# A two-layer decoder trunk on one core: the first stage's normalised input made by ScalarE, two weight pieces shifted, six more filling products

## The chip, the cores and the metric

The kernel runs on one core of one Trainium2 chip. The metric is device time in microseconds (us) of one execution, lower is better. An execution's time is the span from the first to the last instruction and a little around it: the profiled execution took 977.15 us, of which the span is 975.3 us.

## The reference

One sequence of 256 tokens, width 1024, goes through two layers. Each layer is a half-step gated feed-forward network (FFN), an attention and a second half-step FFN. Before each of them the residual is normalised and modulated with numbers made from a conditioning vector c. The part that the change touches is the very first of these:

```python
def rms_norm(x, g):
    xf = x.astype(jnp.float32)
    y = xf * lax.rsqrt(jnp.mean(xf * xf, axis=-1, keepdims=True) + EPS)
    return (y * g.astype(jnp.float32)).astype(x.dtype)

def modulate(h, shift, scale):
    return h * (1 + scale[:, None, :]) + shift[:, None, :]

def swiglu(h, w_in, w_out):
    g, u = jnp.split(h @ w_in, 2, axis=-1)
    return (jax.nn.silu(g) * u) @ w_out

c_act = jax.nn.silu(c)
mod = c_act @ ada_w[layer] + ada_b[layer]
sh1, sc1, g1, sh2, sc2, g2, sh3, sc3, g3 = jnp.split(mod, N_MOD, axis=-1)
h = modulate(rms_norm(x, norm_g[layer, 0]), sh1, sc1)
x = x + 0.5 * g1[:, None, :] * swiglu(h, ffn_w_in[layer, 0], ffn_w_out[layer, 0])
```

All weights are float32 in HBM, some 260 MB with the matrices that make `mod`.

## The kernel before, in words

**Split products.** Every large product is made of three matmuls (`mm3`, line 410). A float32 number is written as a high part rounded to TensorE's format (fp32r) plus a low part, the remainder rounded. The three are high weight times high input, low weight times high input, high weight times low input; low times low is dropped. The names are `wh`, `wl` for a weight piece and `HH`, `HL` for the normalised input. Each of the three has 128 weight columns as its stationary operand and 256 tokens as the moving one.

**The stream of weight pieces.** All weight matrices form one list of pieces of 128 x 1024 numbers (or less), loaded in order by SP's queue into six buffers `raw` (`w_dma`, line 287). ScalarE (ACT) rounds a piece to `wh` (`cp_part`, line 298, six buffers); VectorE (DVE) subtracts, `wl = raw - wh` (`sub_part`, line 310, five buffers); TensorE (PE) uses them up. A piece is 24 matmuls. A `raw` buffer is free, and its next transfer issued, when its `wl` has been made. A dictionary `shift` (line 268) starts a few pieces, the first ones of a stage, 16 numbers (64 bytes) further on in their buffer.

**The modulation numbers.** The rows of the matrices that give `mod` come in units of 1 MB, `ada`, into three buffers. `ada_block` (line 196) handles half a unit, 128 outputs: one DVE instruction multiplies it by `cact` and sums (with a second one, DVE_READ_ACCUMULATOR, that reads the sum out). For a scale the block then makes `A = (1 + scale) * g`, the norm's weight times the modulation. In the first stage this is done for each column at once, by a DVE instruction on 128 x 1 numbers. After the second half of a unit SP is asked for the next one.

**The first stage.** The first FFN starts before anything is known: x, c and the weights are still arriving. So its first 16 column blocks (`win0`, K0 = 4 groups of gate and up) go over all 8 chunks of the contraction, `for k in range(NC)` in `ffn` (line 576), with all 8 PSUM banks as accumulators, `pf0` to `pf7`. A turn k has 48 matmuls and needs two weight pieces, 2k and 2k+1, one `ada` unit (scale and shift of chunk k) and the chunk's input. `make_h` (line 467) makes that: DVE writes `ht = x * A * r`, where r is the reciprocal root mean square; ACT writes `HH = ht + shift`, rounded; DVE writes `HL = (ht + shift) - HH`. The first piece's `cp_part` stands ahead of the loop (line 929).

**After the loop.** ACT loads the table for Silu, rounds two further pieces, and then reads the accumulators: `sg = silu(pf0)` on ACT, then `hf = sg * pf1` on DVE (`evac`, line 562), and so on for four pairs. The next group's accumulators `pg4` and `pu4` lie in the banks of `pf0` and `pf1` (one pool of four banks, tag `mm`), so they can't be written before `sg` and `hf` have read these.

**The order.** Each engine runs its instructions in the order of the program. In the first stage that order is the order of the code. After it a planner decides (class `InOrder`, line 54, and `bg`, line 378): a rough clock for each engine, with costs per instruction, places the rounding, subtracting and `ada_block` work between the others. A change in the first stage thus changes the planner's clocks and, a little, what it places where later on. PE's order is written out by hand and has no such freedom.

**Filling products.** `warm(n)` (line 896) issues n products of a constant tile with itself on PE, which nothing reads, while PE would wait; six of them stand just ahead of the first stage.

Of the kernel before, what the change touches and what calls it, by code (L numbers as in the profile page):

```python
# [10 lines left out]
F32 = mybir.dt.float32  # L11
F32R = mybir.dt.float32r
BF16 = mybir.dt.bfloat16
AF = mybir.ActivationFunctionType
# [89 lines left out]
def trunk(ctx, tc, a, out):  # L104
# [91 lines left out]
    def ada_block():  # L196

        u, i = divmod(ada_done[0], 2)
        if u >= len(ada_list):
            return  # L200
        ada_done[0] += 1
        t = ada_tiles[u]
        m, j = ada_list[u][i]
        if m not in mods:
            mods[m] = [mod_col(), None]
        mt = mods[m][0]
        col = V_ADAB + 2 * u + i
        dve.tensor_tensor_reduce(
            t[:, i], t[:, i], cact, 1.0, vecs[:, col:col + 1], ALU.mult, ALU.add,
            accum_out=mt[:, j:j + 1])  # L210
        kind = m[1] % 3 if m[0] != "kv" else m[1]
        if kind != 0 and m[1] != 5:
            if mods[m][1] is None:
                mods[m][1] = mod_col()
            mx = mods[m][1]
            js = (j, j + 1) if m == (0, 1) else ((j - 3, j + 1) if j % 4 == 3 else None)
            if js is not None:
                js = slice(*js)
                if kind == 1:
                    gc = V_KVN if m[0] == "kv" else V_NORM + (m[0] * 3 + m[1] // 3) * NC  # L220
                    dve.scalar_tensor_tensor(
                        mx[:, js], mt[:, js], 1.0, vecs[:, gc + js.start:gc + js.stop],
                        op0=ALU.add, op1=ALU.mult)
                else:
                    dve.tensor_scalar_mul(mx[:, js], mt[:, js], 0.5)
        if i == 1:
            ada_dma()
# [45 lines left out]
        shift[first] = 16  # L273
    first = next(p for p, v in enumerate(pieces) if v[0].tensor is a["wlast"].tensor)
    shift.update({p: 32 if p > first else 16 for p in range(first, len(pieces))})
    gated = [None]
    raws, his, los = [], [], []
    taken = [0]
# [19 lines left out]
    def cp_part():  # L298

        u = len(his)  # L300
        n = pieces[u][2]
        act.t = max(act.t, used[u - NHI] if u >= NHI else 0.0)
        raw = raws[u]
        if u >= len(pieces) - 6:
            gated[0](raw[:, :n])
        wh = wp.tile([P, WB], F32R, tag="wh", name="wh")[:, shift.get(u, 0):]
        act.plainly(lambda: act.copy(wh[:, :n], raw[:, :n]))
        his.append(wh)
# [158 lines left out]
    def make_h(k, r, m):  # L467

        A, sh = mods[m[0]][1], mods[m[1]][0]
        t = kp.tile([P, S], F32, tag="ht", name=f"ht{k}")  # L470
        dve.scalar_tensor_tensor(t, x[k], A[:, k:k + 1], r, op0=ALU.mult, op1=ALU.mult)
        hh, hl = hn[k]
        act.activation(hh, t, AF.Identity, bias=sh[:, k:k + 1])
        return lambda: dve.scalar_tensor_tensor(hl, t, sh[:, k:k + 1], hh.bitcast(F32),
                                                op0=ALU.add, op1=ALU.subtract)

    class MakeH:


# [68 lines left out]
    def ffn(l, i, kind, m, nxt, at=2):  # L548
# [24 lines left out]
        if (l, i) == (0, 0):  # L573
            banks = ([mmbank(f"pf{b}") for b in range(4)] + [sbank(f"pf{b}") for b in range(4, 6)]
                     + [abank("pf6"), bbank("pf7")])
            for k in range(NC):
                if k:
                    ada_block()
                    cp_part()
                    ada_block()  # L580
                f = make_h(k, kind, m)
                sub_part()
                cp_part()
                f()
                sub_part()
                blk = take("win0")
                for b in range(4 * K0):
                    mm3(banks[b // 2][:, (b % 2) * 256:(b % 2) * 256 + 256], blk(b * P), hn[k],
                        k == 0 and b % 2 == 0, k == NC - 1)
            table(AF.Silu)  # L590
            cp_part()
            sub_part()
            cp_part()
            sub_part()
            mode[0] = "run"
            for j in range(K0):
                if j < 2:
                    evac(banks[2 * j], banks[2 * j + 1])
                    if j == 0:
                        flush()  # L600
                        flush()
                else:
                    later(2 * j - 2, lambda j=j: evac(banks[2 * j], banks[2 * j + 1]))
            j0 = K0
        elif kind == "late":
            banks = [mmbank("lg0"), mmbank("lg1"), sbank("lu0"), sbank("lu1")]
            r = None
            for kh in range(2):
                blk = take("win")
                for kk in range(4):  # L610
                    k = kh * 4 + kk
                    for b in range(4):
                        mm3(banks[b][:, :SX], blk(kk * 512 + b * P), hx[k], k == 0, k == NC - 1)
                    if k == 2:
                        r = rstd_of(AF.Silu)
                        mh = MakeH(r, m)
                    elif 2 < k < 7:
                        if k == 6:
                            cp_part()
                        mh.go(2 if k < 6 else 1)  # L620
            sub_part()
            mh.go(2)
            mode[0] = "run"
            sg = kp.tile([P, 512], F32, tag="w512a", name="sg")
            hf = kp.tile([P, 512], F32, tag="w512b", name="hf")
            cols = []

            def late_block(b):
                if b == 0:
                    cols.append(late_cols(banks))  # L630
                c = cols[0]
                t = kp.tile([P, S], F32, tag="sq", name=f"lt{b}")
                dve.tensor_tensor(t, banks[b][:, :S], r, op=ALU.mult)
                cs = slice((b % 2) * S, (b % 2) * S + S)
                if b < 2:
                    act.activation(sg[:, cs], t, AF.Silu, bias=c[:, b:b + 1])
                else:
                    dve.scalar_tensor_tensor(hf[:, cs], t, c[:, b:b + 1], sg[:, cs],
                                             op0=ALU.add, op1=ALU.mult)
                if b == 3:  # L640
                    hid_out(hf)
            for b in range(4):
                later(2 + b, lambda b=b: late_block(b))
            j0 = 1
# [251 lines left out]
    def warm(n):  # L896

        pw = bbank("warm")
        for _ in range(n):
            mm(pw[:, :P], ones, ones, start=True, stop=True)  # L900
# [24 lines left out]
    ada_block()  # L925
    ada_block()
    rstd = rstd_of(None, [sq4[i][:, h * S:(h + 1) * S] for i in (0, 2) for h in range(2)])
    warm(6)
    cp_part()


# [572 lines left out]
```

## Time and profile before

| | |
|---|---|
| median of 3 runs | 973.57 us |
| the runs | 970.95, 977.09, 973.57 us |
| profiled execution | 977.15 us |
| its span | 975.3 us |
| granted TensorE clock | 0.998 (1.00 in every stretch from 10 us on) |
| busy: PE / DVE / ACT / POOL | 99% / 84% / 57% / 7% |
| 128 x 256 matmuls of fp32r, mean | 277 to 278 ns each, about 113 to 118 ns from start to start |
| first stage (turns 0 to 7) on PE | 13.8 to 60.5 us |

How to read it: matmuls are pipelined, so a row's duration (0.28 us) is longer than the distance to the next row's start, and it is the distance that counts. The same is true on DVE and ACT, by some hundredths of a microsecond: what an instruction costs in a full queue is the distance to the next start. The page's share of 99% for PE therefore doesn't say that PE is at its peak, only that something is nearly always in it.

### The profile page before, as it was taken

How to read it: one execution, taken by the hardware profiler on the slowest of the kernel's cores; microseconds unless marked ns; L12 is line 12 of the kernel's file. 1: busy time of each engine (PE TensorE's matmuls, PEld its weight loads, DVE VectorE, ACT ScalarE, POOL GpSimd, SP SyncE). 2: the span in 40 equal slices, each digit the busy share in tenths (PEclk: the TensorE clock that was granted, in tenths of full speed). 3: DMA queues.
4: the chain of work that ended last, by engine and by line, in shares of the span. 5: the costliest groups of instructions: out<-in, count | busy, mean ns of one | idle time of the engine just before them, and what ended most of it. 6: DMA issues, size and time to landing. Idle time of an engine off the chain costs nothing.

```text
span 975.3 us, 20416 instructions
## 1 busy us (share of the span) xinstructions
PE 964.5 (99%) x8076; PEld 937.8 (96%) x8076; DVE 822.0 (84%) x1372; ACT 551.3 (57%) x894; POOL 67.5 (7%) x110
## 2 busy tenths in 40 slices
PE   8999999999999999999999999999999999999997
PEld 6999999998999999999998999999998899999997
DVE  7989979989999998878889989888988799555575
ACT  5465545666787644445567554545567776555432
POOL 0000100000112000000000000000034013300000
PEclk9999999999999999999999999999999999999999
DMA  9988999968767699878959799988996337977651
GB/s 361 414 352 279 332 361 341 356 224 277 288 212 252 201 379 373 289 257 301 318 186 376 272 353 336 365 295 307 331 297 195 105 117 214 279 155 270 185 152 44
DMA packets 69473, 268.22 MB, mean 275 GB/s; under 512 B 9417, under 2 KB 10225, under 8 KB 59266
## 3 DMA queue, kind: packets, MB, share of 16 engines
q1 hardware_dynamic: 66016, 259.69, 76.3%
q0 software_dynamic: 3072, 6.92, 2.4%
q8 instruction: 63, 1.03, 0.4%
q10 hardware_dynamic: 290, 0.32, 0.1%
q14 instruction: 32, 0.26, 0.1%
HBM read 264.75 MB, written 2.66 MB: 274 GB/s over the span
## 4 chain that ended last, share of the span: by engine, by line
PE 96%; DVE 2%; ACT 1%; DMA 1%; issue 0%; POOL 0%; SPq 0%; DVEq 0%; ACTq 0%
PE po L99 25%; PE pg L99 21%; PE pu L99 21%; PE pf L99 5%; PE pv L99 5%; PE lp L99 4%; PE pqk L99 3%; PE pw L99 3%; PE lq L99 1%; PE lu L99 1%; PE lg L99 1%; PE pk L99 1%; DVE ada L99 1%; PE wb L99 1%; DMA ada<-in_ada 1%; PE sb L99 1%
## 5 line engine op out<-in xcount | busy, mean ns | idle before, releaser
L99 ACT CAST wh<-raw 128x1024 fp32r<-128x1024 f32 (+1 forms) x360 | 346.8, 973 | 213.7 <-PE pu L99 84.8
L99 DVE TENSOR_TENSOR wl<-raw,wh 128x1024 fp32r<-128x1024 f32 (+1 forms) x360 | 399.7, 1128 | 75.6 <-ACT sg L99 20.7
L99 DVE CUSTOM_DVE_ANT_0 ada<-ada,cact,vecs 128x1024 f32<-128x1024 f32 x160 | 203.5, 1279 | 0.3 <-DMA ada<-in_ada 0.3
L99 PE MATMUL pg<-HH,wl 128*128 128x256 f32 x608 | 168.8, 278 | 0.0
L99 PE MATMUL pg<-HH,wh 128*128 128x256 f32 x608 | 168.7, 278 | 0.0
L99 PE MATMUL pu<-HH,wh 128*128 128x256 f32 x608 | 168.6, 277 | 0.0
L99 PE MATMUL pu<-HL,wh 128*128 128x256 f32 x608 | 168.6, 277 | 0.0
L99 PE MATMUL pg<-HL,wh 128*128 128x256 f32 x608 | 168.6, 277 | 0.0
L99 PE MATMUL pu<-HH,wl 128*128 128x256 f32 x608 | 168.6, 277 | 0.0
L99 PE MATMUL po<-hidh,wh 128*128 128x256 f32 x528 | 146.6, 278 | 0.0
L99 PE MATMUL po<-hidh,wl 128*128 128x256 f32 x528 | 146.6, 278 | 0.0
L99 PE MATMUL po<-hidl,wh 128*128 128x256 f32 x528 | 146.6, 278 | 0.0
L99 PEld LDWEIGHTS pg<-HH,wl 128*128 128x128 f32 x608 | 114.7, 189 | 0.1
L99 PEld LDWEIGHTS pg<-HH,wh 128*128 128x128 f32 x608 | 114.2, 188 | 0.7 <-issue 0.6
L99 PEld LDWEIGHTS pu<-HH,wl 128*128 128x128 f32 x608 | 114.7, 189 | 0.0
L99 PEld LDWEIGHTS pu<-HL,wh 128*128 128x128 f32 x608 | 114.1, 188 | 0.0
L99 PEld LDWEIGHTS pg<-HL,wh 128*128 128x128 f32 x608 | 114.1, 188 | 0.0
L99 PEld LDWEIGHTS pu<-HH,wh 128*128 128x128 f32 x608 | 114.1, 188 | 0.0
L99 PEld LDWEIGHTS po<-hidh,wl 128*128 128x128 f32 x528 | 99.9, 189 | 0.0
L99 PEld LDWEIGHTS po<-hidh,wh 128*128 128x128 f32 x528 | 99.1, 188 | 0.0
L99 PEld LDWEIGHTS po<-hidl,wh 128*128 128x128 f32 x528 | 99.1, 188 | 0.0
L99 ACT CAST hidh<-hf 128x512 fp32r<-128x512 f32 x44 | 27.3, 621 | 41.2 <-DVE hf L99 41.0
(224 smaller groups left out, 1849.1 us busy)
## 6 DMA issues: line engine op xcount, KB each, us to landing
raw<-in_win SPq DMA_DIRECT2D x176, 512.0 KB, 6.9
ada<-in_ada SPq DMA_DIRECT2D x79, 1024.0 KB, 7.2
raw<-in_wout SPq DMA_DIRECT2D x48, 384.0 KB, 5.6
raw<-in_wout SPq DMA_DIRECT2D x48, 320.0 KB, 5.8
raw<-in_wqk SPq DMA_DIRECT2D x16, 512.0 KB, 5.4
raw<-in_wo SPq DMA_DIRECT2D x16, 512.0 KB, 5.1
raw<-in_wlast SPq DMA_DIRECT2D x16, 512.0 KB, 4.4
raw<-in_wv SPq DMA_DIRECT2D x8, 512.0 KB, 7.3
```

The source lines that it names most:

```text
L99: return self.tc.keep_in_program_order(f(*args, **kw))
```

## The change

Four edits, all in the first stage or ahead of it.

1. `ada_block`: for the first norm of layer 0, `A` is made by ACT (`Identity` of `mt * g + g`) and no longer by DVE.
2. `make_h_first` takes the place of `make_h` in the loop over k. ACT makes h twice: `HH`, rounded, as before, and `h` in float32. DVE then only subtracts, `HL = h - HH`, from two tiles.
3. For k = 0 one more `cp_part` stands ahead of `make_h_first`; every later rounding in the loop is thereby one piece further on than before.
4. `shift` also holds pieces 4 and 10, the first pieces of turns 2 and 5; and `warm(6)` becomes `warm(12)`.

```diff
@@ ada_block
                 if kind == 1:
                     gc = V_KVN if m[0] == "kv" else V_NORM + (m[0] * 3 + m[1] // 3) * NC
+                    g = vecs[:, gc + js.start:gc + js.stop]
+                    if m == (0, 1):
+                        act.activation(mx[:, js], mt[:, js], AF.Identity, bias=g, scale=g)
+                        return
                     dve.scalar_tensor_tensor(
-                        mx[:, js], mt[:, js], 1.0, vecs[:, gc + js.start:gc + js.stop],
-                        op0=ALU.add, op1=ALU.mult)
+                        mx[:, js], mt[:, js], 1.0, g, op0=ALU.add, op1=ALU.mult)
@@ shift
     shift.update({p: 32 if p > first else 16 for p in range(first, len(pieces))})
+    shift.update({2 * k: 16 for k in (2, 5)})
@@ beside make_h
+    def make_h_first(k, r, m):
+
+        A, sh = mods[m[0]][1], mods[m[1]][0]
+        t = kp.tile([P, S], F32, tag="ht", name=f"ht{k}")
+        dve.scalar_tensor_tensor(t, x[k], A[:, k:k + 1], r, op0=ALU.mult, op1=ALU.mult)
+        hh, hl = hn[k]
+        act.activation(hh, t, AF.Identity, bias=sh[:, k:k + 1])
+        h = kp.tile([P, S], F32, tag="sq", name=f"h{k}")
+        act.activation(h, t, AF.Identity, bias=sh[:, k:k + 1])
+        return lambda: dve.tensor_tensor(hl, h, hh.bitcast(F32), op=ALU.subtract)
@@ ffn, the first stage's loop
                     ada_block()
                     cp_part()
                     ada_block()
-                f = make_h(k, kind, m)
+                if k == 0:
+                    cp_part()
+                f = make_h_first(k, kind, m)
                 sub_part()
                 cp_part()
                 f()
@@ ahead of the first stage
-    warm(6)
+    warm(12)
```

The order that comes out of it is shown at two places. The first is DVE in the first turn and the start of the second; `ht`, `HL` and `wl` are as above, `ISA ada` is the product and sum of half a unit, `ISA modall` reads it out, and `SCALAR_TENSOR_TENSOR modall` is `A`. Before:

```order
L99 SCALAR_TENSOR_TENSOR ht0_171<-x_78,modall_91,r0_148 128x256
L99 TENSOR_TENSOR wl_174<-raw_97,wh_161 128x1024
L99 SCALAR_TENSOR_TENSOR HL_93<-ht0_171,modall_91,HH_92 128x256
L99 TENSOR_TENSOR wl_181<-raw_99,wh_178 128x1024
L99 ISA ada_101,modall_91<-ada_101,cact_89,vecs_76 128x1024
L99 ISA modall_91 128x1
L99 SCALAR_TENSOR_TENSOR modall_91<-modall_91,vecs_76 128x1
L99 ISA ada_101,modall_91<-ada_101,cact_89,vecs_76 128x1024
L99 ISA modall_91 128x1
```

And the same place in the change:

```order
L99 SCALAR_TENSOR_TENSOR ht0_179<-x_78,modall_91,r0_148 128x256
L99 TENSOR_TENSOR wl_184<-raw_97,wh_167 128x1024
L99 TENSOR_TENSOR HL_93<-h0_182,HH_92 128x256
L99 TENSOR_TENSOR wl_191<-raw_99,wh_177 128x1024
L99 ISA ada_101,modall_91<-ada_101,cact_89,vecs_76 128x1024
L99 ISA modall_91 128x1
L99 ISA ada_101,modall_91<-ada_101,cact_89,vecs_76 128x1024
L99 ISA modall_91 128x1
```

`A` has left DVE, and `HL` reads `h0`, which ACT has to make first. Every turn is changed in this way.

The second place is ACT at the end of the first stage, from the last turn's `HH` to the first read of an accumulator. `CAST` is `cp_part`, and the `raw` that it reads tells the piece. Before, piece 15 is `raw_459`, piece 16 `raw_521`, piece 17 `raw_528`, piece 18 `raw_590`:

```order
L99 ACTIVATE HH_92<-ht7_654,modall_91 128x256
L99 CAST wh_661<-raw_459 128x1024
L99 ACT_TABLE_LOAD
L99 CAST wh_717<-raw_521 128x1024
L99 CAST wh_723<-raw_528 128x1024
L99 ACTIVATE sg_729<-pf0_163 128x512
L99 CAST wh_735<-raw_590 128x1024
```

In the change piece 15 is `raw_477`, piece 16 `raw_541`, piece 17 `raw_548`, piece 18 `raw_612`:

```order
L99 CAST wh_671<-raw_477 128x1024
L99 ACTIVATE HH_92<-ht7_676,modall_91 128x256
L99 ACTIVATE h7_679<-ht7_676,modall_91 128x256
L99 CAST wh_685<-raw_541 128x1024
L99 ACT_TABLE_LOAD
L99 CAST wh_741<-raw_548 128x1024
L99 CAST wh_747<-raw_612 128x1024
L99 ACTIVATE sg_753<-pf0_169 128x512
```

The casts of pieces 15 to 17 each stand one place earlier, and the cast of piece 18 now stands ahead of `sg` on the first accumulator instead of behind it. The third place is DVE right after that, from the last `HL` of the first stage. In the change:

```order
L99 TENSOR_TENSOR HL_93<-h7_679,HH_92 128x256
L99 TENSOR_TENSOR wl_688<-raw_477,wh_671 128x1024
L99 TENSOR_TENSOR wl_743<-raw_541,wh_685 128x1024
L99 TENSOR_TENSOR wl_749<-raw_548,wh_741 128x1024
L99 TENSOR_TENSOR wl_756<-raw_612,wh_747 128x1024
L99 TENSOR_TENSOR hf_755<-sg_753,pf1_170 128x512
L99 ISA ada_532,modall_91<-ada_532,cact_89,vecs_76 128x1024
```

Before, the fourth `wl` (of piece 18) stood behind `hf`, and the first `ada` block of the next stage some fifteen rows later. PE's order is the same but for the six filling products. From here to the end DVE and SP have the same work in a slightly other order, with a few `ada` blocks placed earlier or later.

## The prediction

> **What bounds the kernel now.** I read the page's totals first, then the chain of waits, then the timeline of the first stage engine by engine, and last a table by stretches. The profiled execution took 977.15 us: a span of 975.3 us and 1.85 us around it.
>
> ```profile
> span 975.3 us, 20416 instructions
> PE 964.5 (99%) x8076; PEld 937.8 (96%) x8076; DVE 822.0 (84%) x1372; ACT 551.3 (57%) x894; POOL 67.5 (7%) x110
> ```
>
> PE sets the time nearly everywhere. Something changed in the first stage counts only if it lets PE reach the next stage earlier. The chain in order of time (start, length, engine, matmuls) shows the turns as PE has them, each counted from its third product:
>
> ```profile
> 14.79 5.73 PE pf L99 x48
> ...
> 54.99 5.69 PE pf L99 x46
> ```
>
> From 14.79 to 54.99 are seven turns of 5.74 us. Is that PE's own pace? The third product of the last turn on PE, and a whole turn on DVE (start, length, engine, operation; the distance to the next start is the cost):
>
> ```profile
> 54.99 0.39 PE L99 MATMUL pf<-HL,wh 128*128 128x256 f32 x1
> ```
> ```profile
> 49.18 1.23 DVE L99 TENSOR_TENSOR wl<-raw,wh 128x1024 fp32r<-128x1024 f32 x1
> 50.32 1.28 DVE L99 CUSTOM_DVE_ANT_0 ada<-ada,cact,vecs 128x1024 f32<-128x1024 f32 x1
> ...
> 51.64 0.16 DVE L99 SCALAR_TENSOR_TENSOR modall<-modall,vecs 128x1 f32<-128x1 f32 x1
> 51.72 1.28 DVE L99 CUSTOM_DVE_ANT_0 ada<-ada,cact,vecs 128x1024 f32<-128x1024 f32 x1
> ...
> 52.92 0.48 DVE L99 SCALAR_TENSOR_TENSOR ht<-x,modall,r 128x256 f32<-128x256 f32 x1
> 53.32 1.22 DVE L99 TENSOR_TENSOR wl<-raw,wh 128x1024 fp32r<-128x1024 f32 x1
> 54.46 0.48 DVE L99 SCALAR_TENSOR_TENSOR HL<-ht,modall,HH 128x256 fp32r<-128x256 f32 x1
> 54.93 1.23 DVE L99 TENSOR_TENSOR wl<-raw,wh 128x1024 fp32r<-128x1024 f32 x1
> ```
>
> No: PE's third product waits until `HL`, started at 54.46, is written, and DVE goes from `wl` at 49.18 to `wl` at 54.93, 5.75 us, without a gap. DVE bounds the first stage, by 0.3 us a turn over PE at 113 ns a product (48 x 0.1132 = 5.43 us). The stretches (length, PE busy and products, PEld, DVE, ACT, POOL, clock, DMA share, GB/s) show two more things:
>
> ```profile
> 50.00:60.00 10.00, 9.99 (x86) 9.79 (x86) 8.83 (x13) 6.27 (x8) 0.00 (x0) 1.00 1.02 414
> 60.52:63.37 2.85, 2.85 (x27) 2.85 (x26) 2.85 (x4) 2.57 (x5) 0.00 (x0) 1.00 1.03 411
> 64.00:106.00 42.00, 42.00 (x373) 42.00 (x373) 37.05 (x49) 24.09 (x29) 0.00 (x0) 1.00 0.80 271
> 110.00:196.00 86.00, 86.00 (x761) 86.00 (x760) 74.89 (x112) 44.48 (x63) 4.19 (x8) 1.00 0.96 353
> 318.00:326.00 8.00, 8.00 (x73) 8.00 (x72) 7.13 (x14) 5.07 (x12) 0.00 (x0) 1.00 0.39 131
> 330.00:500.00 170.00, 170.00 (x1443) 169.95 (x1442) 146.12 (x206) 87.39 (x113) 1.63 (x3) 1.00 0.89 312
> 545.00:715.00 170.00, 170.00 (x1502) 170.00 (x1501) 153.45 (x215) 85.76 (x108) 0.00 (x0) 1.00 0.91 327
> ```
>
> First, the DMA engines are full during the first stage. Second, PE has two paces for the same kind of matmul at a full clock and without a gap: 170/1502 = 113.2 ns, and 170/1443 = 117.8 ns through the second FFN. At 318 that FFN is still fast (8.00 us for some 71 products, two of the 73 being left over from ahead of the window); it changes at a wait:
>
> ```profile
> 326.03 0.28 PE L99 MATMUL pg<-HH,wh 128*128 128x256 f32 x1
> 326.19 0.39 PE L99 MATMUL pg<-HH,wl 128*128 128x256 f32 x1
> ```
>
> The slow pace costs 174 x (1 - 113.2/117.8) = 6.8 us from there to 500 alone. The three runs lie 6.1 us apart, about one such stretch, and the profiled run is at the slow end, 3.6 us above the median. So I make the sum against 977.15 and carry only the difference to the median.
>
> **The change part by part.** *DVE's turn.* `A` goes, and with it the distance from the first `ada` block to the second falls from 51.72 - 50.32 = 1.40 to what a block costs that is followed by something else, 52.92 - 51.72 = 1.20. `HL` becomes a subtraction of two tiles, for which the residual sums are the nearest row:
>
> ```profile
> 171.85 0.42 DVE L99 TENSOR_TENSOR acc<-acc,sq 128x256 f32<-128x256 f32 x1
> 172.19 0.82 DVE L99 TENSOR_TENSOR wl<-raw,wh 128x640 fp32r<-128x640 f32 x1
> ```
>
> That is 0.34 against 54.93 - 54.46 = 0.47 now. The turn is then wl 1.14, two blocks 2.40, `ht` 0.40, `wl` 1.14, `HL` 0.34, 5.42 us, where it was 5.75. PE's own 5.43 takes over: 0.31 a turn less, 2.1 us over seven.
>
> *ACT's turn.* It gains `h`, 128 x 256, bounded by `HH`'s row below (0.41 to the next start, 0.51 in all), and `A`, 128 x 1, for which the nearest row is 0.21:
>
> ```profile
> 324.40 0.21 ACT L99 COPY lcol<-lg 128x1 f32<-128x1 f32 x2
> ```
>
> With two casts of 1.04 that is 3.2 of 5.43 us. `h` is done 0.51 + 0.41 + 0.51 = 1.43 us after `ht` starts, and DVE turns to `HL` 0.40 + 1.14 = 1.54 after it: it fits by 0.1. Because the cast of the next piece stood between `HH` and DVE's second `wl`, moving the casts one place ahead also frees that step.
>
> *The start.* The extra cast stands ahead of the first `HH`:
>
> ```profile
> 11.05 1.04 ACT L99 CAST wh<-raw 128x1024 fp32r<-128x1024 f32 x1 [0.18 <-DMA raw<-in_win]
> 13.25 0.51 ACT L99 ACTIVATE HH<-ht,modall 128x256 fp32r<-128x256 f32 x1 [1.15 <-DVE ht L99]
> ```
> ```profile
> L99 SPq DMA_DIRECT2D raw<-in_win x2: 499/546/592, 2.9 to 3.6; - x2
> DMA to landing us min/median/max: 8.1/8.4/8.7
> ```
>
> Piece 1 was issued at 3.6 and landed 8.7 later, at 12.3; its cast ends at 13.3. `A` off DVE brings `ht` 0.2 forward, so `HH` could have run at 13.05 and now runs at 13.3: level with before. With `h` done 0.92 after that, at 14.2, `HL` can start where it did (14.79 less the last turn's 54.99 - 54.46, 14.26), and is 0.13 shorter; but I count half of that, since ACT is now just in time. Start: -0.07 us, bounds -0.2 and +0.3.
>
> *Filling products.* Twelve of them are 24 rows of 0.112, 2.7 us from 10.19, done at 12.9, ahead of the first `HH` (13.25), for which PE has to wait anyway:
>
> ```profile
> 10.19 1.50 PE L99 MATMUL warm<-ones 128*128 128x128 f32 x12
> ```
>
> The clock was 1.00 across the gap before, so I price them at nothing.
>
> *The shifted pieces.* The stretch at 60.52 is a shifted piece: 24 products in 2.85 us, 119 ns. Turns 2 and 5 get one such piece each. Against the fast pace that costs 24 x 5.6 ns = 0.13 us a turn; where the turn would have been slow, 48 x 4.6 ns = 0.22 can come back if the other piece turns fast. Between -0.2 and +0.13 a turn; I take +0.13, since with the slow wait gone I expect fast turns. The Trainium skill ("TensorE: Matmul & The Clock Gate", Part 2, step 1) says that PE has two independent read ports, so that loading weights doesn't slow the matmul that streams; by that an address could matter to neither, and this term would be 0. The two paces in the rows, at one form, speak against it.
>
> *What is late next.* With PE through its last turn at 14.72 + 7 x 5.43 + 0.26 + 46 x 0.1132 = 58.2 instead of 60.5, 2.3 us earlier, the next group's `pg4` and `pu4` need the banks of `pf0` and `pf1`. Before, `sg` and `hf` had read these in time:
>
> ```profile
> 53.44 0.51 ACT L99 ACTIVATE HH<-ht,modall 128x256 fp32r<-128x256 f32 x1 [3.34 <-DVE ht L99]
> 53.85 1.04 ACT L99 CAST wh<-raw 128x1024 fp32r<-128x1024 f32 x1
> 54.91 1.28 ACT L99 ACT_TABLE_LOAD   x1
> 56.20 2.00 ACT L99 CAST wh<-raw 128x1024 fp32r<-128x1024 f32 x2
> 58.11 0.59 ACT L99 ACTIVATE sg<-pf 128x512 f32<-128x512 f32 x1
> ```
> ```profile
> 59.56 0.68 DVE L99 TENSOR_TENSOR hf<-sg,pf 128x512 f32<-128x512 f32 x1
> ```
> ```profile
> 60.52 0.28 PE L99 MATMUL pg<-HH,wh 128*128 128x256 f32 x1
> ...
> 61.23 0.28 PE L99 MATMUL pu<-HH,wh 128*128 128x256 f32 x1
> ```
>
> In the change the cast of piece 18 stands ahead of `sg`. Piece 18 is the transfer issued at 48.83:
>
> ```profile
> L99 SPq DMA_DIRECT2D raw<-in_win x1: 327/327/327, 48.8 to 48.8; - x1
> DMA to landing us min/median/max: 8.9/8.9/8.9
> ```
>
> It landed at 57.7. In the change it is issued some 2 us earlier, but the engines ahead of it are full (share 1.02, 414 GB/s), and the same bytes stand ahead of it, so I expect it at 57.7 again. Then: cast until 58.75, `sg` 58.7 to 59.3, and `pg4` waits about 1.0 us. DVE's order has `wl` of piece 18 ahead of `hf` too: `wl` from 58.8, `hf` 59.95 to 60.63, and `pu4` starts at 60.65 instead of 61.23. Behind the waiting cast on ACT stand `sg` and all later casts; PE is the one who waits. Of 2.3 us, 0.6 stays.
>
> *After that* PE runs product to product (170.00 busy of 170.00), with `wl` made five pieces ahead, so 0.6 us is carried to the end; the few `ada` blocks placed elsewhere lie on a DVE busy 146 of 170. Sum: 977.15 - 0.6 = 976.6 for an execution like the profiled one, 973.57 - 0.6 = 973.0 for the median.
>
> **The rivals.** *Piece 18 is not late.* If it lands by 56, the whole 2.3 us stays: 971.3. For it: it is issued 2 us earlier. Against: the full engines. The Trainium skill ("DMA: Bandwidth & Descriptors", Where 436 GB/s comes from) has a ceiling of 435 GB/s; at that rate the bytes between 11.0 and 57.7 would be there at 55.4, an estimate, and this rival would hold. The rows have 414.
>
> *The slow stretch doesn't come.* The wait at 326 is of 0.2 us, and the order around it hardly changes, but whether the pace changes there is not in the order. Without it: 976.6 - 6.8 = 969.8. For it: the fastest run before, 970.95, can hardly have had one.
>
> *Slower: the new wait leaves PE at the slow pace.* `pg4`'s wait of 1 us is of the kind after which the pace changed at 326, and here everything from 64 to 196, at the fast pace now (42/373, 86/761), hangs on it: 128 x (117.8/113.2 - 1) = 5.2 us, median 973.0 + 5.2 = 978.2. It decides from 0.6/0.0046 = 130 products on, a tenth of the stretch. Against it: the piece at 60.52 is a shifted one and came out at the fast pace.
>
> *No change in time:* `h` late or the casts starved, DVE's turn not shorter: 973.6.
>
> **How the numbers follow.** Forecast 0.45 (973.0; its own range 970 to 977, the spread of the runs), piece 18 in time 0.15 (971.3), no slow stretch 0.15 (969.8), slow after the new wait 0.2 (978.2), no change 0.05 (973.6). The range 968.5 to 978.5 takes in all of these with the 1 us that the start and the shifts leave open; outside lie tails of the forecast's spread and two stretches at once. One per cent, 9.7 us, is what a measurement of this kernel can tell from no change: below 963.8 no single case reaches (0.02), above 983.3 only two new slow stretches together (0.04).
>
> **What would show it.** Right: turns of 5.4 to 5.5 us from third product to third product; DVE idle somewhere in the stage; the cast of piece 18 waiting for `DMA raw` up to about 57.7; PE idle about 1 us at the first `pg` and half of that at the first `pu`, which starts near 60.6. Wrong: `pg` straight behind `pf` at 58.2 (piece 18 in time); turns still of 5.7 (`HL` waiting for ACT); in the stretches, a count of products in 110 to 196 near 730 instead of 761, or one near 1,500 in 330 to 500.

## The result, and the profile after

The change took 970.10 us (median of 22 runs, 969.51 to 972.09), before took 971.43 us (22 runs, 970.79 to 977.09). The ratio is 0.9984 (95% interval 0.9978 to 0.9991), some 1.3 to 1.5 us less: clear of the noise, well under the 1% that the prediction asked of a change, and inside its range. The three runs of before that were known ahead (970.95, 973.57, 977.09) gave a median 2.1 us above that of 22.

The profiled execution of the change took 971.33 us. First its totals:

```profile
span 969.6 us, 20460 instructions
PE 960.7 (99%) x8088; PEld 934.9 (96%) x8088; DVE 819.4 (85%) x1364; ACT 558.9 (58%) x910; POOL 67.5 (7%) x110
```

ACT has 7.6 us more (551.3 before), DVE 2.6 less. One turn on DVE, in its timeline:

```profile
47.52 1.22 DVE L99 TENSOR_TENSOR wl<-raw,wh 128x1024 fp32r<-128x1024 f32 x1
...
52.61 0.42 DVE L99 TENSOR_TENSOR HL<-h,HH 128x256 fp32r<-128x256 f32 x1
52.94 1.22 DVE L99 TENSOR_TENSOR wl<-raw,wh 128x1024 fp32r<-128x1024 f32 x1
```

From 47.52 to 52.94 are 5.42 us, and `HL` costs 52.94 - 52.61 = 0.33. The end of the first stage, on ACT, DVE and PE (in brackets the idle time ahead of an instruction, and what ended it):

```profile
57.68 1.05 ACT L99 CAST wh<-raw 128x1024 fp32r<-128x1024 f32 x1 [1.62 <-DMA raw<-in_win]
58.64 0.59 ACT L99 ACTIVATE sg<-pf 128x512 f32<-128x512 f32 x1
```
```profile
58.77 1.23 DVE L99 TENSOR_TENSOR wl<-raw,wh 128x1024 fp32r<-128x1024 f32 x1 [1.45 <-ACT wh L99]
59.91 0.68 DVE L99 TENSOR_TENSOR hf<-sg,pf 128x512 f32<-128x512 f32 x1
```
```profile
59.32 0.35 PE L99 MATMUL pg<-HH,wh 128*128 128x256 f32 x1
59.50 0.28 PE L99 MATMUL pg<-HH,wl 128*128 128x256 f32 x1
...
60.65 0.39 PE L99 MATMUL pu<-HH,wh 128*128 128x256 f32 x1 [0.39 <-DVE hf L99]
```

ACT waits 1.62 us for the transfer of piece 18 with `sg` behind it, DVE 1.45 for that cast with `hf` behind it, and `pu4` starts at 60.65 instead of 61.23. PE had come to this place at 59.3 instead of 60.5. The stretches (length, PE busy and products, PEld, DVE, ACT, POOL, clock, DMA share, GB/s) of this profile:

```profile
64.00:106.00 42.00, 42.00 (x359) 42.00 (x359) 38.01 (x51) 23.16 (x29) 0.00 (x0) 1.00 0.82 295
...
330.00:485.00 155.00, 155.00 (x1369) 155.00 (x1368) 137.94 (x194) 80.30 (x104) 1.05 (x2) 1.00 0.91 327
```

From 330 on PE is at the fast pace, 155/1369 = 113.2 ns, where before's profile has 1,319 products in the same window, 117.5. From 64 to 106 it is at the slow one, 42/359 = 117.0, where before had 112.6; it runs product to product in both. The 5.8 us between the two profiled executions are therefore mostly a slow stretch that is gone (5.9 us by two landmarks shown further down, where the prediction had 6.8: its window to 500 us counted wide products from 493 us on as slow ones) and one that is new (42 x (1 - 112.6/117.0) = 1.6 us of it in this window), and say little about the change. A second profile of the change, further down, has neither.

### The profile page after: what moved, and what is told of

It reads as the page before. It is cut to its first block, busy times and chain, and to the rows that moved or that the text cites. A ratio compares the mean times of both kernels' runs of the same rounds, so it can differ in the third digit from the quotient of the medians.

```text
span 969.6 us, 20460 instructions
## 1 busy us (share of the span) xinstructions
PE 960.7 (99%) x8088; PEld 934.9 (96%) x8088; DVE 819.4 (85%) x1364; ACT 558.9 (58%) x910; POOL 67.5 (7%) x110
## 4 chain that ended last, share of the span: by engine, by line
PE 94%; DVE 3%; DMA 1%; ACT 1%; issue 0%; ACTq 0%; SPq 0%
PE po L99 25%; PE pu L99 21%; PE pg L99 21%; PE pw L99 5%; PE pv L99 5%; PE lp L99 4%; PE pqk L99 3%; DVE wl L99 2%; PE lq L99 1%; DVE ada L99 1%; PE lu L99 1%; PE lg L99 1%; PE pk L99 1%; DMA raw<-in_win 1%; PE wb L99 1%; PE sb L99 1%
```

## The experiments

All times are medians. Before was run beside each series and took 971.3 to 971.5 us; ratios are to it, with 95% intervals.

### What sets the start of `pu4`

**The cast of piece 18 put behind `sg`.** After the loop one pair of calls changes:

```diff
             table(AF.Silu)
             cp_part()
             sub_part()
-            cp_part()
             sub_part()
             mode[0] = "run"
```

> The change, but the rounding of weight piece 18 stands behind the first sg (silu of pf0) on ScalarE, and its low part behind the first hf on VectorE. Everything later in the stream of pieces is one cast later. Theory (the cast of piece 18, which waits for its transfer until 57.6 us, is what holds pu4 at 60.65): sg runs at about 56.1, hf at 57.0 to 57.6, and PE goes from pf to pg4 to pu4 without a wait, pu4 0.7 us behind pg4. With pf ending at 59.3 as in the profile of the change that is 0.65 us earlier, with pf ending at 58.2 to 58.7 it is 1.3 to 1.7 earlier: 968.4 to 969.5 us against 970.1. Rival (what the two waits take is given back or lost later, for instance because without them PE goes on at another pace): 970.1 or more, the first pu4 early all the same.

969.77 us (968.97 to 972.33), ratio 0.9983 (0.9974 to 0.9991). ACT, and then PE, in its profile:

```profile
56.02 0.59 ACT L99 ACTIVATE sg<-pf 128x512 f32<-128x512 f32 x1
57.72 1.05 ACT L99 CAST wh<-raw 128x1024 fp32r<-128x1024 f32 x1 [1.11 <-DMA raw<-in_win]
```
```profile
59.33 0.28 PE L99 MATMUL pg<-HH,wh 128*128 128x256 f32 x1
...
60.04 0.28 PE L99 MATMUL pu<-HH,wh 128*128 128x256 f32 x1
```

The cast waits for piece 18 until 57.72 as before, but nothing is held up by it. `pu4` follows `pg4` at six products' distance and starts 0.61 us earlier than in the change, as the theory had it. The median is 0.33 us lower than the change's, with overlapping intervals: by itself not settled by the times. The profiled execution, 972.33, was the slowest of the series; it has a slow stretch of its own, from 144 to 198 us, behind a wait of 0.09 us. The expectation's rival, that the gain is lost again later, is half true: this edit also brings back before's order of later work, and the landmarks further down show what that costs.

**Without the shifts of pieces 4 and 10.**

```diff
-    shift.update({2 * k: 16 for k in (2, 5)})
```

> The change without the shift of pieces 4 and 10; the order of all instructions is that of the change. Theory (piece 18 sets the start of pu4, PE's pace in turns 2 and 5 doesn't): no products at 119 ns among turns 1 to 7, pf ends at 58.2 to 59.3, pu4 still at 60.6 to 60.7, time 970.1 +- 0.4. Rival (the shifts are what gained: without them PE keeps a slow pace through the turns or takes it into the stretch from 64 us on): 971 to 972, and pf ending after 59.3.

969.79 us (969.70 to 971.74), ratio 0.9984 (0.9976 to 0.9993): the same as the change. The turns in its profile, and `pu4`:

```profile
16.00:56.00 40.00, 40.00 (x342) 40.00 (x341) 38.92 (x57) 26.36 (x38) 0.00 (x0) 1.00 1.02 414
```
```profile
59.83 0.27 PE L99 MATMUL pg<-HH,wh 128*128 128x256 f32 x1
...
60.71 0.39 PE L99 MATMUL pu<-HH,wh 128*128 128x256 f32 x1
```

40/342 = 117.0 ns and no idle time (two or three of the products counted are left over from ahead of the window, here and in the other short windows): PE ran all the turns at the slow pace, 48 products in 5.6 us, and not at DVE's 5.42. It came to `pg4` at 59.83, half a microsecond later than in the change, and `pu4` starts where it started in the change all the same. A slower PE cost nothing, since piece 18 sets that start.

**A back on VectorE.**

```diff
-                    if m == (0, 1):
-                        act.activation(mx[:, js], mt[:, js], AF.Identity, bias=g, scale=g)
-                        return
```

> The change with A back on VectorE (the small instruction of 0.2 us a turn); h on ScalarE, the extra cast, the shifts and the filling products as in the change. Theory (in the change the end of the first stage is set by piece 18 and not by the turns): VectorE's turn is 5.62 us, pf ends at 59.5 to 60.1 instead of 59.3, but pu4 starts at 60.6 to 60.8 all the same: 970.1 +- 0.4. Rival (the turns decide): 1.4 us later at pu4, 971.0 to 971.6.

969.99 us (969.70 to 972.00), ratio 0.9991 (0.9982 to 0.9999). DVE's turn and `pu4`:

```profile
42.59 1.22 DVE L99 TENSOR_TENSOR wl<-raw,wh 128x1024 fp32r<-128x1024 f32 x1
...
48.20 1.21 DVE L99 TENSOR_TENSOR wl<-raw,wh 128x1024 fp32r<-128x1024 f32 x1
```
```profile
60.65 0.39 PE L99 MATMUL pu<-HH,wh 128*128 128x256 f32 x1 [0.27 <-DVE hf L99]
```

The turn is 5.61 us, 0.19 longer than in the change, and `pu4` starts at 60.65 to the hundredth. In the change as it stands, moving `A` is worth nothing. (The profiled execution, 972.00, was the slowest of the series: behind `pu4` it is at the slow pace, with 359 products from 64 to 106 us, the same count as in the change's first profile.)

**Both: `sg` first, and no shifts.**

> Both: sg ahead of the cast of piece 18, and no shifted pieces 4 and 10. Theory: PE passes the group boundary without waits, so now the pace in the turns counts in full: at 113 ns pf ends at 58.2 to 58.6 and the time is 968.2 to 968.8; if turns are at 118 ns it is that plus up to 1.5 us. Rival: as with sg first alone, 970 or more.

969.16 us (968.94 to 970.65), ratio 0.9979 (0.9971 to 0.9988). In the profiled execution (970.64) PE was at the slow pace through the turns and came to `pu4` at 60.67 without a wait:

```profile
16.00:56.00 40.00, 40.00 (x342) 40.00 (x341) 39.41 (x58) 26.77 (x39) 0.00 (x0) 1.00 1.02 413
```
```profile
60.67 0.28 PE L99 MATMUL pu<-HH,wh 128*128 128x256 f32 x1
```

In this execution, with piece 18 out of the way, PE's own pace is the bound, and at 117 ns it takes up nearly all that the earlier `sg` had freed. It was one of the two slowest of the series; the median is 0.9 us below the change's, and what PE did in an ordinary execution of this kernel no profile shows.

**`sg` first, and only piece 1 shifted.** If the pace is what is left, a shifted piece behind the last wait of the start should free it:

```diff
-    shift.update({2 * k: 16 for k in (2, 5)})
+    shift[1] = 16
```

> sg ahead of the cast of piece 18, and of the shifted pieces of the first stage only piece 1 (in turn 0) instead of 4 and 10. Theory (PE's pace in the turns is what is left between 5.42 and 5.65 us a turn, and a shifted piece behind the last wait sets it to 113 ns): piece 1 at 119 ns, everything from piece 2 to the end of pf at 113, pf ends at 58.1 to 58.5 and pu4 starts at 58.8 to 59.2, where the profile of sg first without shifts had 60.67; 968.0 to 968.8 us. Rival (VectorE's turn or the landing of the pieces makes PE wait in the turns after all, or the gain is lost at the next wait): pf after 59.3, 969.1 or more.

969.00 us (six runs, 968.76 to 969.18), ratio 0.9972 (0.9961 to 0.9983). Every one of its runs is below the fastest of all 30 runs of the change (969.47). The turns, and `pu4`:

```profile
21.00:57.00 36.00, 36.00 (x320) 36.00 (x319) 35.22 (x51) 23.67 (x34) 0.00 (x0) 1.00 1.02 414
```
```profile
59.44 0.28 PE L99 MATMUL pu<-HH,wh 128*128 128x256 f32 x1
```

36/320 = 112.5 ns: fast from piece 2 to the end. `pu4` starts 1.2 us earlier than in the change, although this execution's first product was late (14.18). It missed the expected 58.8 to 59.2 by about that late start, and the expected 968.0 to 968.8 by a little. Of the kernels here it is the one with the best ratio to before, but the interval overlaps with that of the kernel without shifts (969.16 us): the trace shows what piece 1 does to the pace, the times alone don't settle what it is worth.

### The parts of the edit

**Without the extra cast ahead of the loop.**

```diff
-                if k == 0:
-                    cp_part()
                 f = make_h_first(k, kind, m)
```

> The change without its extra rounding ahead of the loop, so each cast in the loop stands where it stood before, behind HH and now h; A and h stay on ScalarE, HL stays a subtraction. Theory (the offloading shortens VectorE's turn only together with the cast one piece ahead): from the start of ht, HH comes at 0.51, h at 0.92, the cast of piece 2k+1 at 1.33 and ends at 2.4, while VectorE would take its second wl at 0.40 + 1.14 + 0.34 = 1.9. It waits 0.5 us a turn: turns of about 5.9 us where they were 5.75 before and 5.42 in the change; pf ends near 61.5 and the time is 971.5 to 972.7. Rival (the offloading alone does it): turns of 5.43 to 5.65, and since piece 18's cast isn't ahead of sg here, pu4 right behind pg4: 969.8 or less.

972.72 us (972.29 to 975.18), ratio 1.0014 (1.0005 to 1.0023): slower than before. DVE, then ACT:

```profile
50.85 1.23 DVE L99 TENSOR_TENSOR wl<-raw,wh 128x1024 fp32r<-128x1024 f32 x1 [0.45 <-ACT wh L99]
...
56.80 1.23 DVE L99 TENSOR_TENSOR wl<-raw,wh 128x1024 fp32r<-128x1024 f32 x1 [0.44 <-ACT wh L99]
```
```profile
55.33 0.49 ACT L99 ACTIVATE h<-ht,modall 128x256 f32<-128x256 f32 x1
55.73 1.03 ACT L99 CAST wh<-raw 128x1024 fp32r<-128x1024 f32 x1
```

DVE does less and its turn is longer, 5.95 us from `wl` to `wl`: `h` pushes the cast on ACT 0.4 us back, and DVE waits 0.45 for it. The extra cast isn't an addition to the offloading but its condition.

**Before, with twelve filling products.**

```diff
-    warm(6)
+    warm(12)
```

> The kernel before with twelve filling products where it had six, nothing else. Theory (the filling products lie in a wait for HH and cost nothing): 971.4 +- 0.4, ratio 1.000. Since 20 of 22 runs of before lie from 970.8 to 973.3, this profile should also show what an ordinary execution of before looks like: the second FFN at the fast pace (about 1,500 products from 330 to 500 us, not 1,443), and the span near 969.6. Rival: twelve products change the clock or the start and carry a part of the gain of the change: 970.1 to 970.7. Second rival: the slow stretch belongs to before always, then 1,443 again at about 971.

971.43 us, ratio 0.9994 (0.9982 to 1.0007): nothing, as expected. Its profile (971.17 us) has the second FFN at the fast pace, so the slow stretch from 326 us on in the first profile of before was that execution's own; `pu4` starts at 61.15, close to the 61.23 there:

```profile
330.00:485.00 155.00, 155.00 (x1369) 155.00 (x1369) 138.83 (x195) 81.23 (x104) 1.06 (x2) 1.00 0.90 325
```

### The two paces

**No shifts at all.** The shifted pieces at the head of the four FFN stages go too:

```diff
-        shift[first] = 16
...
-    shift.update({2 * k: 16 for k in (2, 5)})
```

> The change with no shifted pieces at all ahead of the last FFN's output: neither 4 and 10 nor the four that before has at the head of its stages (60, 329, 538, 806 us). Theory (PE's two paces are a state that a wait sets by chance and that lasts until the next wait or shifted piece): one or more of the stretches 60 to 196, 330 to 485, 539 to 714 and 806 to 900 run at 118 ns from end to end in most executions, 5 to 7 us each: 975 to 990, and widely spread runs. Rival (the shifts don't set the pace): all stretches as they were, 969.3 to 970.3, less 0.13 us for each shifted piece.

Six of ten runs took 969.04 to 969.52 us, the others 971.27, 974.50, 976.26 and 977.50; the median is 969.43 and the ratio 0.9997 (0.9978 to 1.0016). The profiled execution was one of the first kind, and the first of the long stretches, with no shift ahead of it, is at 132/1161 = 113.7 ns; the others are as fast:

```profile
64.00:196.00 132.00, 132.00 (x1161) 131.23 (x1160) 116.50 (x173) 72.94 (x98) 4.87 (x9) 1.00 0.94 337
```

So most executions don't need the shifts, and some lose 2 to 8 us without them; that these had a slow stretch is a reading of their times, not of a profile. The theory's "in most executions" was wrong. That a wait can set the pace is seen in the turns of this execution: PE is at the fast pace up to 25 us, waits there, and is at the slow pace from there to the end of the first stage.

**The change again.**

> The change itself, a second profile. Its first profile (971.33 us) had the slow pace from 59.6 to 108 us behind the wait at pu4, its median is 970.1. Theory (that stretch is one execution's chance, worth 410 x 4.7 ns = 1.9 us, and the ordinary execution doesn't have it): 61 to 196 at 113 ns, 1,176 products or so at the fast pace, pu4 at 60.6 to 60.7, 969.5 to 970.2. Rival (the wait at pu4 inside the shifted piece leaves PE slow in the change always): the slow stretch again, 971 or more.

970.10 us (8 runs, 969.47 to 972.54), ratio 0.9986 (0.9970 to 1.0002). The stretch behind `pu4` is fast here, and the turns show what shifted pieces do: from 16 to 28 us slow, between pieces 4 and 10 fast, behind piece 10 fast:

```profile
64.00:106.00 42.00, 42.00 (x373) 42.00 (x372) 38.35 (x51) 24.84 (x31) 0.00 (x0) 1.00 0.87 304
```
```profile
16.00:28.00 12.00, 12.00 (x104) 12.00 (x103) 11.80 (x18) 7.05 (x11) 0.00 (x0) 1.00 1.02 416
30.00:42.00 12.00, 12.00 (x109) 12.00 (x108) 12.00 (x18) 7.47 (x12) 0.00 (x0) 1.00 1.02 414
46.00:58.00 12.00, 12.00 (x108) 12.00 (x107) 10.56 (x14) 7.81 (x11) 0.00 (x0) 1.00 1.02 416
```

In the first profile of the change piece 4, from 26 to 28.7 us, was met at the fast pace and left at the slow one, and piece 10 the other way round:

```profile
16.00:25.00 9.00, 9.00 (x82) 9.00 (x81) 9.00 (x15) 6.11 (x10) 0.00 (x0) 1.00 1.01 412
29.00:42.00 13.00, 13.00 (x112) 13.00 (x112) 13.00 (x21) 8.29 (x13) 0.00 (x0) 1.00 1.02 413
46.00:58.00 12.00, 12.00 (x108) 12.00 (x108) 10.52 (x14) 7.92 (x11) 0.00 (x0) 1.00 1.02 415
```

So the rival that the wait at `pu4` always leaves PE slow falls, and with it any fixed price of the wait.

**The second FFN's shift moved five pieces ahead**, into the last of the wide products (258 columns), beside `sg` first and piece 1:

```diff
-        shift[first] = 16
+        shift[first - 5 if (l, i) == (0, 1) else first] = 16
```

> As sg first with piece 1 shifted, and besides, the shifted piece of the second FFN is no longer the one at 329 us but the last of the wide products (258 columns) at 315, five pieces earlier. Theory: those products run at 120 ns whatever their address, so the shift is free there, and the products from 317 to 329 run at 113 ns at once: 0.13 us for the piece at 329, and up to 96 x 4.7 ns = 0.45 where that stretch was slow, 0.1 to 0.6 less than with piece 1 alone. Rival (a shift among wide products doesn't set the pace): 317 to 485 at the pace that the wait before it left, up to 1,470 x 4.6 ns = 6.8 us more.

968.77 us (12 runs, 968.50 to 975.58), ratio 0.9979 (0.9967 to 0.9992), not to be told from the kernel above by the ratios. Twelve wide products in a row, then the stretch behind, with piece 1 alone:

```profile
314.20 0.28 PE L99 MATMUL lu<-HH,wl 128*128 128x258 f32 x1
...
315.53 0.28 PE L99 MATMUL lu<-HH,wh 128*128 128x258 f32 x1
```
```profile
317.00:327.00 10.00, 10.00 (x87) 10.00 (x87) 9.09 (x18) 6.96 (x14) 0.00 (x0) 1.00 0.39 129
```

And with the moved shift:

```profile
314.25 0.29 PE L99 MATMUL lu<-HL,wh 128*128 128x258 f32 x1
...
315.64 0.29 PE L99 MATMUL lu<-HH,wl 128*128 128x258 f32 x1
```
```profile
317.00:327.00 10.00, 10.00 (x90) 10.00 (x90) 9.09 (x18) 6.97 (x14) 0.00 (x0) 1.00 0.41 129
```

The pace behind it is fast at once (90 products in 10 us against 87), but the shift isn't free as expected: the wide products are 1.39/11 = 0.126 us apart with it and 1.33/11 = 0.121 without. In these two executions nothing of the gain is left at the end of that FFN: its last product starts 0.5 us earlier with the moved shift (484.47 against 484.98), but PE then waits for ACT's `HH`, and the next group starts at 485.10 against 485.09.

**A shifted piece in the first attention's output projection**, once in the best kernel and once in before. These products go in threes, from three pieces in turn:

```diff
         shift[first] = 16
+        if (l, i) == (0, 1):
+            shift[first - 9] = 16
```

> As sg first with piece 1 shifted, and besides, the last of the eight weight pieces of the first attention's output projection (used at 295 to 303 us, three products in nine) lies 64 bytes further on. In the profiles of the kernels with sg first, and in that of before with twelve filling products, everything from 295 to 330 ran at 118 ns; in those of the change and of the change without shifts it ran at 113 outside the wide products. Theory (this is the same latched pace, set at the waits ahead of 295, and it is worth 170 products x 4.7 ns = 0.8 us): with the shift the products from 298 on, and those from 315 to 329, run at 113, for 24 x 6 ns = 0.14 us of its own: 968.3 to 968.6 against 969.0. Rival (a shifted piece in groups of three doesn't set the pace, or slows the others): 969.0 to 969.3.

> The kernel before with that same one piece of the first attention's output projection shifted, nothing else. Theory (before usually runs at 118 ns from 295 to 330 and the change usually doesn't, and so 0.7 to 0.8 us of the measured 1.3 to 1.5 comes from there and only 0.5 from the first stage): 970.6 to 970.9 against 971.5, the first stage as before with pu4 at 61.2. Rival (the difference arises elsewhere): 971.4 to 971.6.

969.08 us (968.69 to 970.77), ratio 0.9976 (0.9965 to 0.9988), and 971.26 us (970.46 to 978.20), ratio 1.0003 (0.9985 to 1.0020). Neither moved. Six microseconds of these products, in the first of the two:

```profile
297.00:303.00 6.00, 6.00 (x53) 6.00 (x53) 4.85 (x13) 5.30 (x11) 1.21 (x2) 1.00 1.01 384
```

53 in 6 us where piece 1 alone had 54 and the kernel with the moved shift 56; before has 53 from 299 to 305 us with the shift and with twelve filling products alone. One shifted piece in groups of three didn't set the fast pace, so this couldn't test how much of the difference between the change and before lies there; the landmarks in the next section can.

## Why the prediction was right, and where it was not

**The range held**, but it was 10 us wide, so this says little. The predicted 973.0 was 2.9 us above the result. 2.1 of these are its base, the median of three runs; the change itself was put at -0.6 and measured -1.3 to -1.5. As shown below, the first stage gave 0.3 to 0.4 us, where 0.6 was forecast, and the rest came from a place where the prediction expected nothing.

**DVE's turn.** Right: 5.42, and `HL` 0.33 for 0.34.

**ACT's turn.** Fit as forecast, and that the earlier casts are a condition was shown by taking them away. `A` was mis-sized:

```profile
10.01 0.39 ACT L99 ACTIVATE modall<-modall,vecs 128x1 f32<-128x1 f32 x1 [0.60 <-DVE modall L99]
```

0.39 us and not the 0.21 of the copy that I took as the nearest row. The Trainium skill ("ScalarE: Activation LUTs", What ACT_TABLE_LOAD costs) gives an ACTIVATE 186 ns and some 93 more for each scale or bias that is read from a column of memory, by estimate 0.37 us for this one, and the row agrees. ACT had the room.

**The start.** Mis-sized, and for a reason that isn't the change's. The eight products of `psn`, on PE, in the change's first profile and in before's (durations shortest/median/longest in ns, first and last start):

```profile
L99 PE MATMUL psn<-sqs,ones x8: 634/634/635, 7.5 to 10.5; 128*128 128x256 f32 x8
```
```profile
L99 PE MATMUL psn<-sqs,ones x8: 379/574/634, 7.5 to 10.0; 128*128 128x256 f32 x8
```
```profile
10.90 3.23 PE L99 MATMUL warm<-ones 128*128 128x128 f32 x24
```

In the change's first profile the eight took 3.4 us to the start of the next product, a filling one (10.90), and in before's 2.7, where the last of them were already quicker. `HH`, which needs their result, came 0.36 later (13.61 for 13.25). In the other profiles the filling products begin anywhere between 10.37 and 10.90, whatever was edited, and the first product of `pf` starts between 13.77 and 14.18. What differs from one execution to the next is the moment at which PE's clock steps up: the clock record in the trace begins, at full clock, 9.46 us into before's span, 11.70 into that of the change's first profile, and between 9.8 and 12.2 in the others. (The views print 1.00 ahead of that too, where nothing is on record.) The Trainium skill ("TensorE: Matmul & The Clock Gate", Part 1, What's actually happening) says that the window which decides it runs freely and doesn't begin with the kernel, so that the step comes at another place in each run; the records agree. -0.07 with bounds to +0.3 should have had this spread as its bounds. With 24 filling rows the cover was all but gone in that execution (they end at 14.13, `HH` at 14.12); it still cost nothing.

**PE's 5.43 takes over.** Half right. DVE stopped being the bound, but what took over was PE at either of its paces, 5.43 or about 5.63 us a turn. "With the slow wait gone I expect fast turns" is the step that failed: without a wait the pace that PE has after the start stays, and in the profile without the shifts of pieces 4 and 10 that was the slow one for all seven turns. In the change's first profile the turns are between 5.44 and 5.68 us, by the pace that they ran at, where 5.4 to 5.5 was the sign of being right. `pf` ended at 59.3 to 59.8 and not at 58.2: in that profile 0.4 of the 1.1 is the late start, the rest the slow turns.

**The shifted pieces.** +0.13 each was the price of their 119 ns, but not what matters about them, which is the pace that they leave behind. In the change's two profiles pieces 4 and 10 were met at the slow pace twice, and left fast both times; met at the fast pace twice, and left slow once. The Trainium skill ("TensorE: Matmul & The Clock Gate", Part 2, step 1) says that loading weights takes no read bandwidth from the running matmul. It says nothing of addresses; that an address could then matter to neither was the prediction's own inference, and these rows are against it. Their sum in the change was nothing, since piece 18 sets the end.

**What is late next.** Right, and to the hundredth at the place that counts: piece 18's cast at 57.68 (57.7), `sg` 58.64, `hf` 59.91 (59.95), `pu4` 60.65 (60.65). `pg4` hardly waited (its second product comes 0.18 us behind the first) instead of 1.0, because PE itself came later. The rival "piece 18 is not late" fell. Its transfer, in the change:

```profile
L99 SPq DMA_DIRECT2D raw<-in_win x1: 328/328/328, 47.3 to 47.3; - x1
DMA to landing us min/median/max: 10.2/10.2/10.2
```

It was issued 1.5 us earlier than before (48.8) and took 10.2 us instead of 8.9, so it landed no earlier, as the prediction had argued from the full engines. It took the edit of `sg` to get round it.

**The slow wait as a rival.** It happened in the first profile, 1.6 us from 64 to 106, a third of its 5.2, not in the second, and again in that of `A` back on VectorE: it comes in some executions and not in others. **The slow stretch in the second FFN** did not come, in this or any later profile: it belonged to a rare execution of before, and I took that execution as the base. The prediction had named it as a sign of being wrong, a count near 1,500 from 330 to 500 us: there are 1,493, and 1,493 in before with twelve filling products too.

**From `pu4` on.** Carried 0.6 us to the end, I said; measured are 1.3. Two landmarks, the first product of the group `lp` behind the first FFN (at 197 us) and behind the second (at 486), in the profile of before with twelve filling products and in that of the change without its shifts:

```profile
197.54 0.28 PE L99 MATMUL lp<-HH,wh 128*128 128x258 f32 x1
...
487.01 0.28 PE L99 MATMUL lp<-HH,wh 128*128 128x258 f32 x1
```
```profile
197.19 0.28 PE L99 MATMUL lp<-HH,wh 128*128 128x258 f32 x1
...
485.59 0.28 PE L99 MATMUL lp<-HH,wh 128*128 128x258 f32 x1
```

At 197 this kernel is 0.35 us ahead of before, and the change's second profile 0.33: that is what the first stage gave. At 486 they are 1.42 and 0.73 ahead. The rest is no chance of one execution. From the end of the first stage on, the profiles have only two orders of instructions on DVE and ACT: the change's, with the cast of piece 18 ahead of `sg`, and before's, to which the kernels with `sg` first and the one without the extra cast go back. The distance from the first landmark to the second, in us:

| order behind the first stage | distance between the landmarks, one profile each |
|---|---|
| the change's: the change twice, no shift, no shifts at all, `A` on VectorE | 288.39, 289.07, 288.39, 288.31, 288.61 |
| before's: twelve filling products, shifted output projection, no extra cast | 289.47, 289.41, 289.48 |
| before's: `sg` first, the same without shifts, the same with piece 1 | 289.38, 289.35, 289.27 |
| before's, and the slow stretch in the second FFN: the first profile of before | 295.36 |

With the two further shifts of that stretch, in the kernels with `sg` first and piece 1, it is 289.35 (the moved one) and 288.98 (the output projection). Four of these profiles are of one chip and one series: 288.39 (no shift) against 289.47, 289.38 and 289.35. So the change's order of later work is worth 0.2 to 1.2 us by itself, and that is the step that the prediction put at nothing ("the few `ada` blocks placed elsewhere lie on a DVE busy 146 of 170"). Followed product by product, the gain arises between 278 and 333 us, from the first attention's output projection to the start of the second FFN. The change without its shifts has the same order as the change and still differs by 0.69 us from its second profile, so how much an execution gets varies. Which wait the order removes there stays open. Putting `sg` first wins 0.6 us at `pu4` and gives this gain up, which is why its median falls so little; no kernel here has both.

## What to carry to other kernels

Relieving the engine that bounds a stage is worth only what the next wait leaves: look for what is queued ahead of the first reader of the stage's result, and put a cast that waits for a transfer behind it. Then look at what the edit moves later on: here the order behind the stage was worth as much as the stage itself, and only the distance between two fixed products in every profile showed it. When work is moved to an engine that also feeds the first one, what stood behind it there must be moved ahead in the same edit, or the relief turns into a longer wait. And before a change of a few microseconds is forecast or explained, ask how far two executions of one kernel differ, and sum against an ordinary one.

## What the runs showed of the hardware that I had not expected

- PE's two paces at a full clock (113 and 118 ns for the same 128 x 256 product) are a state that can last over a hundred microseconds (155/1319 = 117.5 ns from 330 to 485 us in before's first profile, 113.2 in the others): without a single shifted piece all long stretches ran at 113 in one execution, and other executions of that kernel took 2 to 8 us more.
- A shift of 64 bytes in the stationary operand slows products with 258 moving columns too (0.126 for 0.121 us), and one shifted piece in groups of three among unshifted ones left no lasting pace (53 products in 6 us).
- The moment at which PE's clock steps up lay between 9.46 and 12.18 us of the span in the records of 14 profiles, and the first product of the first stage started between 13.77 and 14.18.
